# Three transformer blocks on one core: a cheaper root, an earlier start, an interleaved MLP start, and VectorE's later work queued behind each norm's root

## The chip, the cores and the metric

The kernel runs on one core of one Trainium2 chip (trn2). The metric is device time in microseconds (us); lower is better. TensorE (PE) does matmuls and transposes, VectorE (DVE) and ScalarE (ACT) do elementwise work, GpSimd (POOL) and SyncE (SP) here mostly issue transfers. Each engine has its own instruction queue and they meet through semaphores.

## The reference

One sequence of 512 tokens and 1024 features, in fp32, goes through three blocks: (1) latent attention with 8 heads and a gated short convolution side by side, then a gated MLP and a per-layer embedding gate; (2) retention with 4 heads and a squared-ReLU MLP; (3) banded attention with 16 heads and another squared-ReLU MLP. Ahead of, behind and inside these stand norms.

```
def _rmsnorm(x, g):
    y = x * lax.rsqrt(jnp.mean(x * x, axis=-1, keepdims=True) + EPS)
    return y * g
# block 1
z = rmsnorm(x, mix_pre_norm) @ w_in               # latents c_q, c_kv, rope keys, convolution inputs
q = rmsnorm(c_q, q_norm) @ w_uq;  kv = rmsnorm(c_kv, kv_norm) @ w_ukv
a = causal_attention(q, kv);  c = short_gated_conv(z)
m = concat(rmsnorm(a, attn_group_norm), rmsnorm(c, conv_group_norm))
x = x + rmsnorm(m @ w_out, mix_post_norm)
h = rmsnorm(x, ffn_pre_norm)
x = x + rmsnorm((silu(h @ w_gate) * (h @ w_up)) @ w_down, ffn_post_norm)
x = x + sigmoid(x @ w_ple_gate) * rmsnorm(p @ w_ple_proj, ple_norm)
# blocks 2 and 3, i = 0, 1
hn = rmsnorm(h, mix_norm_g[i])
h = h + (retention(hn) if i == 0 else chunk_attention(hn))   # retention norms each of its 4 heads
h = h + square(relu(rmsnorm(h, mlp_norm_g[i]) @ w1[i])) @ w2[i]
return rmsnorm(h, final_norm_g)
```

## The kernel before

**Layout.** Activations are kept transposed, features on partitions and the 512 tokens along the free axis. A product runs over eight 128-feature slices of its input. Every fp32 product is made of three matmuls of rounded parts (`mm3`, L147 to L150): L148 high x high, L149 low weight x high activation, L150 high weight x low activation. So a stream of matmuls at L148, L149, L150 is the body of the kernel; only L149 needs the low part `wl` of the weights.

**Weights.** A weight tile is 128 x 1024 fp32. SP loads it (`load_weights`, L134); ACT rounds it to `wh` (L111); DVE subtracts to get `wl` (L108, "the split"). Tiles `wr`, `wh` and `wl` are triple buffered. The two split instructions carry a priority 80 ahead (`HW = 80`).

**Order.** PE's order is written by hand: products are generators that yield after every `mm3` (a "unit" of three matmuls), and `pull(gen, n)` puts n units at that place in PE's queue. On the other engines a scheduler orders the instructions by priority when the program is built, and each queue then runs in that order.

**Norms.** `Norm` sums squares over the features (`square`: ACT squares, DVE adds). `column()` has PE transpose the sum in 128x128 pieces (L240), and `root()` (L245 to L260) makes the inverse root on DVE: one reduction (L247) and eleven small instructions, the last at L259. `spread()` has PE broadcast the result back over partitions (L265), and ACT copies it to `rb`. Between `column()` and `spread()` the code pulls a few units of the next product so that PE has work while DVE makes the root; new weight tiles that begin in this stretch are loaded, and split, by the instructions written there. A `SplitNorm` does the two 256-token halves one after the other.

**Places named below.** The first norm (start of the program), the two norms of the latents (their columns stand directly one after the other), the attention's norm, the two halves of the norm behind the output projection, the norm ahead of the gated MLP, the two halves of the norm behind it, the norm ahead of retention, retention's four head norms, the norms ahead of MLP 0, of the banded attention and of MLP 1, and the two halves of the last norm.

Of the kernel before, what the change touches and what calls it, by code (L numbers as in the profile page):

```python
# [14 lines left out]
P = 128  # L15
# [17 lines left out]
LAT = (6, 6, 12, 6, 5, 8, 2)  # L33
HID = (0, 9)
N_RET = (8, 5)
N_MLP = ((9, 8), (9, 5))
N_CH = (14, 12)
GG = (6, 7, 6)
FIN = (5, 8)
CO = (4, 11)  # L40
PER2 = (10,) * 8 + (13, 10, 9) + (10,) * 5 + (3,)

BIG = 1.0e30
# [17 lines left out]
def kernel(  # L61
# [29 lines left out]
    def small(n=NT, dt=F32, tag="sm"):  # L91
        return spool.tile([P, n], dt, tag=tag, name="small", bufs=12 if tag == "sm" else 4)
# [11 lines left out]
    def add(out, a, b):  # L104
        dve.tensor_tensor(out=out, in0=a, in1=b, op=ALU.add)  # L105
# [60 lines left out]
    def load4(src, n, acts=None, prepare=None, start=0, pool=None):  # L166
        out = []
        for kk in range(start, start + n):
            w = weight_tiles(pool)
            for k in range(2):  # L170
                load_weights(w, src[kk * P:(kk + 1) * P, :], slice(k * T, (k + 1) * T))
                if prepare is not None:
                    acts.append(prepare(2 * kk + k))
            out.append(w[1:])
        return out
# [41 lines left out]
    class Norm:  # L217


        def __init__(self, n, t0=0, nt=NT, acc=None):  # L220
            self.n, self.nt = n, nt
            self.tok = slice(t0 * P, (t0 + nt) * P)
            self.acc, self.r, self.col = acc, None, None
            self.waiting = []

        def square(self, src):
            w = self.nt * P
            if self.acc is None:
                self.acc = tmp()[:, :w]
                act.activation(self.acc, src, AF.Square)  # L230
            else:
                t = tmp()[:, :w]
                act.activation(t, src, AF.Square)  # L233
                add(self.acc, self.acc, t)

        def column(self):
            ps = bank()
# [5 lines left out]

        def root(self, ps):

            a, na, u, h, y, w = (small(dt=d, tag=g)[:, :self.nt] for d, g in ((F32, "sm"),) * 4 + ((I32, "smi"), (F32, "sm")))
            dve.tensor_reduce(out=a, in_=ps.rearrange("p (t f) -> p t f", f=P)[:, :self.nt, :], op=ALU.add, axis=AX.X)  # L247
            dve.tensor_scalar(a, a, 1.0 / self.n, EPS, ALU.mult, ALU.add)
            dve.tensor_scalar(y, a.bitcast(I32), -0.5, 1595932665.0, ALU.mult, ALU.add)
            dve.tensor_scalar(na, a, -0.703952253, None, ALU.mult)  # L250
            y = y.bitcast(F32)
            mul(u, y, y)
            mul(u, u, na)
            dve.scalar_tensor_tensor(out=y, in0=u, scalar=0.703952253 * 2.38924456, in1=y, op0=ALU.add, op1=ALU.mult)
            mul(u, y, y)
            mul(h, u, a)
            dve.tensor_scalar(w, y, 0.375, None, ALU.mult)
            dve.scalar_tensor_tensor(out=h, in0=h, scalar=-10.0 / 3.0, in1=h, op0=ALU.add, op1=ALU.mult)
            dve.scalar_tensor_tensor(out=w, in0=h, scalar=5.0, in1=w, op0=ALU.add, op1=ALU.mult)  # L259
            self.col = w  # L260

        def spread(self, sbuf=True):
            ps = bank()[:, :self.nt * P]
# [17 lines left out]
        def run(self, gen, a=10, b=8):  # L281
            pull(gen, a)
            self.column()
            pull(gen, b)
            self.spread()

    class SplitNorm:
# [128 lines left out]
    for kt in range(KT):  # L416
        t = const.tile([P, T], F32, name=f"x{kt}", tag=f"x{kt}")
        xs.append(t)

    warm = small(1)  # L420
    dve.memset(warm, 0.0)
    copy(warm, warm)
    ident = const.tile([P, P], F32, name="ident", tag="ident")


# [27 lines left out]
    with tc.tile_pool(name="m1", bufs=1) as m1, tc.tile_pool(name="pt1", bufs=1) as ptp:  # L453
# [3 lines left out]

        n_x = Norm(D)
        hn = []
        nc.gpsimd.dma_start(gn, gains)  # L460
        act.dma_start(xs[0], xT[:P, :])

        def first_in(kt):
            if kt > 0:
# [127 lines left out]
        pull(fill, LAT[2])  # L592
        n_lat[0].column()
        n_lat[1].column()
        pull(fill, LAT[3])
        for i in (1, 0):
            n_lat[i].spread()
            nm = ("q_norm", "kv_norm")[i]
# [12 lines left out]
        att = [m1.tile([P, T], F32, name=f"att{i}", tag=f"att{i}") for i in range(4)]  # L611
        wq = [None]
        qs = {}
        n_att = Norm(512)

        def project(h):
            if h == 2:
# [58 lines left out]
        def mla_head(h):  # L676
            def done(po):
                join(att[h // 2][64 * (h % 2):64 * (h % 2) + 64, :], po)
                if h % 2:
                    n_att.square(att[h // 2])  # L680
            return Head(qs.pop(h), keys[h // 2 % 2][h % 2], slice(0, P), causal, 96 ** -0.5, vps, h * P, done, True)

        first = project(0)
# [13 lines left out]
        attention(8, mla_head, mf, lambda h: per[h] if h < 6 else PER[h - 6], ptp, PER[2])  # L697
        pull(mf, OUT[0])
        n_att.column()
        drain(mf)  # L700


        heads = []
        for i in range(4):
            heads.append(split_gain(att[i], g_("attn_gn", i)))

        def out_unit(mt, ps, w, tok):
            yield from units(ps, w, K8[mt % 2 * 4:mt % 2 * 4 + 4], heads, tok=tok)
# [20 lines left out]
                    yield from out_unit(5 + k, ps3[k], ws[k], tok)  # L729

        out = att_out()
        pull(out, OUT[1])
        n_att.spread()
        pull(out, 32 + W_OUT[0] - OUT[1])
        n_post.halves[0].column()
        drain(out)

    ff = tc.tile_pool(name="ff", bufs=3, reuse_waits="tile")
    ffp = ff.__enter__()
# [10 lines left out]
    def boundary(norm, ys, gname, nxt, fill, counts, src, acts, loaded):  # L750

        a, b = norm.halves
        pull(fill, counts[1])
        a.spread(False)
        post_norm_add(a, ys, gname, nxt)
        pull(fill, counts[2])
        banks = [bank() for _ in range(4)]
        first = units4(banks, src, acts, loaded=loaded, tok=a.tok, pool=ffp)
        pull(first, counts[3])
        b.column()  # L760
        pull(first, counts[4])
        b.spread(False)
        post_norm_add(b, ys, gname, nxt)
        drain(first)
        drain(fill)
        return banks, units4(banks, src, acts, loaded=loaded, tok=b.tok)
# [41 lines left out]
    for nh in (8, 8, 6):  # L808
        hid = []
        if h0 == 0:  # L810
            for i in range(2):
                n_x.then(lambda i=i: hidden(hid, banks[i], banks[2 + i]))
            gen = hidden_group(hid, range(2, nh))
            n_x.run(gen, *HID)
            drain(gen)
        else:
            drain(hidden_group(hid, range(h0, h0 + nh)))
        last = h0 + nh == 22
        for mt in range(KT - 3 if last else KT):
            w = weights(rows(w_down, mt, h0, nh), nh * P)  # L820
            ps = bank()
            drain(units(ps, w, K8[:nh], hid))
            if h0 == 0:
                y = ffp.tile([P, T], F32, name=f"f{mt}", tag=f"f{mt}", bufs=1)
                copy(y, ps)
                accs.append(y)
            else:
                add(accs[mt], accs[mt], ps)
            if last:
                n_post.square(accs[mt])  # L830
        if last:
# [12 lines left out]

            drain(down_last(n_post.halves[0]))
            second = down_last(n_post.halves[1])
            pull(second, DOWN[0])
            n_post.halves[0].column()
            drain(second)
        h0 += nh  # L850

    es_t.append(pair())
# [42 lines left out]
    def mlp(i, now, nxt):  # L895
# [8 lines left out]
            hid.append(pr)  # L904

        def group(hid, grp):
            for j in range(8):
                w = weights(rows(m_w1, i * 32 + grp * 8 + j))
                ps = bank()
                yield from units(ps, w, K8, hn)  # L910
                norm.then(lambda ps=ps: square_relu(hid, ps))
                yield
# [22 lines left out]
    def finish(hid, ws):  # L935
# [33 lines left out]
        second = product(b)  # L969
        pull(second, FIN[0])  # L970
        a.column()
        pull(second, FIN[1])
        out = [f32(pair()) for _ in range(KT // 2)]
        output(a, out)
        drain(second)
# [6 lines left out]
    with tc.tile_pool(name="m2", bufs=1, reuse_waits="tile") as m2:  # L982
# [112 lines left out]
        for h in range(4):  # L1095
            if h % 2 == 0:
                ys = []
            vps = values(h)
            pts = retain(h)
            gnorm, os_ = Norm(T), []  # L1100
            gg = gates(h, gnorm, os_, ys)
            pull(gg, GG[0])
            os_ += outputs(vps, pts, gnorm)
            pull(gg, GG[1])
            gnorm.column()
            pull(gg, GG[2])
# [237 lines left out]
```

## Time and profile before

| | |
|---|---|
| three runs | 2006.85, 2009.34, 2009.49 us; median 2009.34 |
| profiled execution | 2007.66 us |
| its span, from first to last instruction | 2005.9 us |
| PE busy | 1967.7 us |
| DVE busy | 1193.7 us |
| ACT busy | 804.8 us |
| mean granted TensorE clock | 0.996 |

The profiled execution's own time is its span and what lies around it. Busy is the time in which an engine executed an instruction; PE's gaps are the difference to the span. The granted clock is 1 at TensorE's full rate (2.4 GHz) and 0.5 at half (1.2 GHz).

### The profile page before, as it was taken

The numbers are of one execution on the slowest core, as the hardware profiler recorded it, in microseconds if no ns is written. First come the engines' busy times: TensorE is split into PE (matmuls) and PEld (weight loads), VectorE is DVE, ScalarE is ACT, GpSimd is POOL, SyncE is SP. The second block draws the span as 40 slices with busy tenths as digits, with TensorE's granted clock in tenths as the row PEclk, the third lists the DMA queues.
The fourth block names the chain that finished last, engine by engine and source line by source line (L and its number), as shares of the span: only waits on it lengthen the run. The fifth ranks groups of instructions, "written<-read, shape, count | busy, mean of one in ns | idle before, by whom it ended". The sixth has DMA issues, their size and how long they took to land.

```text
span 2005.9 us, 23888 instructions
## 1 busy us (share of the span) xinstructions
PE 1967.7 (98%) x9340; PEld 1642.8 (82%) x9340; DVE 1193.7 (60%) x2167; ACT 804.8 (40%) x1298; POOL 10.3 (1%) x22
## 2 busy tenths in 40 slices
PE   8999899999999999999999999999999999999997
PEld 7787888888888788888888888888888878888887
DVE  7978963343469665635566354455598975444354
ACT  5776442332235344333443222223476753222232
POOL 1000000000000000000000000000000000000000
PEclk9999999999999999999999999999999999999999
DMA  5122223233241222222223233323222233233331
GB/s 181 60 65 85 85 86 104 95 95 95 95 129 65 100 75 79 99 99 74 79 95 95 94 95 97 103 95 95 100 85 80 67 107 95 95 95 96 103 95 64
DMA packets 58785, 185.31 MB, mean 92 GB/s; under 512 B 6784, under 2 KB 10000, under 8 KB 58672
## 3 DMA queue, kind: packets, MB, share of 16 engines
q1 hardware_dynamic: 53648, 175.76, 27.3%
q10 hardware_dynamic: 4688, 7.60, 1.3%
q8 instruction: 73, 1.20, 0.3%
q0 software_dynamic: 336, 0.42, 0.1%
q14 instruction: 40, 0.33, 0.1%
HBM read 181.56 MB, written 2.20 MB: 92 GB/s over the span
## 4 chain that ended last, share of the span: by engine, by line
PE 86%; DVE 9%; ACT 3%; issue 1%; DMA 0%; POOLq 0%; POOL 0%; ACTq 0%; DVEq 0%
PE bank L148 28%; PE bank L150 28%; PE bank L149 28%; DVE wl L108 2%; DVE tmp L105 1%; PE bank L360 1%; ACT tmp L328 1%; DVE pair L108 1%; ACT pair L111 1%; PE bank L341 1%; DVE tmp L326 1%; DVE pt L108 1%; ACT wh L111 1%; DVE x L105 0%; DVE pair L121 0%
## 5 line engine op out<-in xcount | busy, mean ns | idle before, releaser
L148 PE MATMUL bank<-pair,wh 128*128 128x512 f32 (+1 forms) x2550 | 979.9, 384 | 9.9 <-ACT pair L120 9.9
L150 PE MATMUL bank<-pair,wh 128*128 128x512 f32 (+1 forms) x2550 | 971.0, 381 | 1.8 <-DVE pair L121 1.5
L149 PE MATMUL bank<-pair,wl 128*128 128x512 f32 (+1 forms) x2550 | 969.5, 380 | 0.0
L111 ACT ACTIVATE wh<-wr 128x1024 fp32r<-128x1024 f32 (+4 forms) x354 | 353.1, 999 | 902.8 <-PE bank L150 654.6
L148 PEld LDWEIGHTS bank<-pair,wh 128*128 128x128 f32 x2550 | 480.9, 189 | 97.2 <-ACT pair L120 11.1
L150 PEld LDWEIGHTS bank<-pair,wh 128*128 128x128 f32 x2550 | 480.5, 188 | 97.0 <-DVE pair L121 3.8
L149 PEld LDWEIGHTS bank<-pair,wl 128*128 128x128 f32 x2550 | 481.0, 189 | 86.5
L108 DVE TENSOR_TENSOR wl<-wr,wh 128x1024 fp32r<-128x1024 f32 (+4 forms) x354 | 405.5, 1146 | 152.9 <-ACT wh L111 152.0
L102 DVE TENSOR_TENSOR tmp<-bank,rb 128x512 f32<-128x512 f32 (+1 forms) x140 | 94.4, 677 | 243.5 <-PE bank L150 238.8
L105 DVE TENSOR_TENSOR x<-x,bank 128x512 f32<-128x512 f32 (+1 forms) x99 | 66.2, 670 | 212.3 <-PE bank L150 212.2
L111 ACT ACTIVATE pair<-tmp 128x512 fp32r<-128x512 f32 (+1 forms) x188 | 118.5, 631 | 103.7 <-DVE tmp L1083 26.1
L108 DVE TENSOR_TENSOR pair<-tmp,pair 128x512 fp32r<-128x512 f32 (+1 forms) x156 | 106.7, 686 | 11.7 <-ACT pair L111 10.8
L105 DVE TENSOR_TENSOR tmp<-tmp 128x512 f32<-128x512 f32 (+1 forms) x107 | 68.2, 641 | 37.2 <-ACT tmp L233 36.7
L148 PE MATMUL bank<-wh,pair 128*128 128x512 f32 x200 | 79.2, 396 | 0.3 <-ACT tmp L111 0.3
L150 PE MATMUL bank<-wl,pair 128*128 128x512 f32 x200 | 78.0, 390 | 0.0
L149 PE MATMUL bank<-wh,pair 128*128 128x512 f32 x200 | 77.9, 389 | 0.0
L328 ACT ACTIVATE tmp<-tmp,small 128x512 f32<-128x512 f32 (+1 forms) x96 | 53.3, 556 | 28.8 <-DVE small L326 27.5
L108 DVE TENSOR_TENSOR pt<-bank,pt 128x512 fp32r<-128x512 f32 (+1 forms) x96 | 42.7, 484 | 10.0 <-ACT pt L111 9.8
L901 DVE SCALAR_TENSOR_TENSOR tmp<-tmp 128x512 f32<-128x512 f32 x64 | 44.2, 692 | 2.1
L120 ACT ACTIVATE pair<-x,gn 128x512 fp32r<-128x512 f32 (+1 forms) x56 | 36.2, 653 | 19.9 <-DVE x L105 18.9
L148 PEld LDWEIGHTS bank<-wh,pair 128*128 128x128 f32 x200 | 37.6, 188 | 7.9 <-ACT tmp L111 0.7
L150 PEld LDWEIGHTS bank<-wl,pair 128*128 128x128 f32 x200 | 37.5, 188 | 7.9
(151 smaller groups left out, 1221.5 us busy)
## 6 DMA issues: line engine op xcount, KB each, us to landing
wr<-in_m_w_dram SPq DMA_DIRECT2D x128, 512.0 KB, 3.7
wr<-in_r_qkg_dram SPq DMA_DIRECT2D x32, 512.0 KB, 3.5
wr<-in_w_gate_dram SPq DMA_DIRECT2D x20, 512.0 KB, 3.5
wr<-in_w_up_dram SPq DMA_DIRECT2D x20, 512.0 KB, 3.5
wr<-in_w_down_dram SPq DMA_DIRECT2D x16, 512.0 KB, 3.5
wr<-in_r_v_dram SPq DMA_DIRECT2D x16, 512.0 KB, 3.4
wr<-in_r_out_dram SPq DMA_DIRECT2D x16, 512.0 KB, 3.6
wr<-in_a_qk_dram SPq DMA_DIRECT2D x16, 512.0 KB, 3.5
```

The source lines that it names most:

```text
L102: dve.tensor_tensor(out=out, in0=a, in1=b, op=ALU.mult)
L105: dve.tensor_tensor(out=out, in0=a, in1=b, op=ALU.add)
L108: dve.tensor_tensor(out=out, in0=a, in1=b, op=ALU.subtract)
L111: act.activation(out, a, AF.Copy)
L120: act.activation(dst[:, 0, tok], src[:, tok], AF.Copy, scale=gain)
L148: pe.matmul(out, lhsT=ah, rhs=bh, start=start, stop=False)
L149: pe.matmul(out, lhsT=al, rhs=bh, start=False, stop=False)
L150: pe.matmul(out, lhsT=ah, rhs=bl, start=False, stop=stop)
L326: dve.tensor_tensor_reduce(out=s[:, :n], in0=ps[:, :n], in1=self.strip[:, T - n:T], scale=-self.scale, scalar=3.0e38, op0=ALU.add, op1=ALU ...
L328: act.activation(s[:, :n], s[:, :n], AF.Exp, bias=self.mx[:, col], scale=-1.0, accum_out=self.sm[:, col])
L341: pe.transpose(pt[:, j * P:(j + 1) * P], s[:, j * P:(j + 1) * P], ident)
L901: dve.scalar_tensor_tensor(out=t, in0=t, scalar=0.0, in1=t, op0=ALU.max, op1=ALU.mult)
```

## The change

1. **Start.** The gains `gn` and the first slice of x are now the first two transfers of ACT's queue (the gains were GpSimd's). The first weight piece is loaded and split as 128 + 384 columns with the first activation's preparation between. Eight matmuls of a zero tile (`IDLE = 8`) stand ahead of PE's first real one.
2. **Root.** `root()` has nine instructions instead of twelve; EPS goes into the sum of squares.
3. **MLP.** The first two tiles of each MLP's first group alternate unit by unit (14 units), and the second MLP's pulls are (14, 6) instead of (9, 5).
4. **Order.** `with norm.first():` is `tc.issue_after(root's last step)`: all that the block writes for DVE stands in DVE's queue behind the last instruction of that root. The blocks enclose the pull between `column()` and `spread()`.
5. **Heads.** The four products of the attention's output with its gain (`split_gain`, one ACT and one DVE instruction each) are made as each pair of heads ends, not together behind the fill.

```
-N_MLP = ((9, 8), (9, 5))
+N_MLP = ((9, 8), (14, 6))
+IDLE = 8
...
     def load4(src, n, acts=None, prepare=None, start=0, pool=None):
...
+                if prepare is not None and kk + k == 0:
+                    load_weights(w, src[:P, :], slice(0, P))
+                    acts.append(prepare(0))
+                    load_weights(w, src[:P, :], slice(P, T))
+                    continue
...
         def square(self, src):
...
-                add(self.acc, self.acc, t)
+                if self.eps:
+                    add(self.acc, self.acc, t)
+                else:
+                    dve.scalar_tensor_tensor(out=self.acc, in0=self.acc, scalar=self.n * EPS / P, in1=t,
+                                             op0=ALU.add, op1=ALU.add)
+                    self.eps = True
...
         def root(self, ps):
-            (12 instructions)
+            dve.tensor_reduce(out=s, in_=ps..., op=ALU.add, axis=AX.X)
+            dve.tensor_scalar(y, s.bitcast(I32), -0.5, 1595932665.0 + half, ALU.mult, ALU.add)
+            y = y.bitcast(F32)
+            stt(out=u, in0=y, scalar=-0.703952253 * 0.375 / n, in1=y, op0=ALU.mult, op1=ALU.mult)
+            mul(u, u, s)
+            stt(out=z, in0=u, scalar=0.375 * 0.703952253 * 2.38924456, in1=y, op0=ALU.add, op1=ALU.mult)
+            stt(out=u, in0=z, scalar=64.0 / (9.0 * n), in1=z, op0=ALU.mult, op1=ALU.mult)
+            mul(u, u, s)
+            stt(out=u, in0=u, scalar=-10.0 / 3.0, in1=u, op0=ALU.add, op1=ALU.mult)
+            self.last = stt(out=w, in0=u, scalar=5.0, in1=z, op0=ALU.add, op1=ALU.mult).ins
...
+        def first(self):
+            return tc.issue_after(self.last)
...
         def run(self, gen, a=10, b=8):
             pull(gen, a)
             self.column()
-            pull(gen, b)
+            with self.first():
+                pull(gen, b)
             self.spread()
...
+    act.dma_start(gn, gains)
+    act.dma_start(xs[0], xT[:P, :])
...
+    for _ in range(IDLE):
+        pe.matmul(zero, lhsT=idle[:, :P], rhs=idle[:, :T], start=True, stop=True)
...
         n_lat[0].column()
         n_lat[1].column()
-        pull(fill, LAT[3])
+        with n_lat[1].first():
+            pull(fill, LAT[3])
...
                 if h % 2:
                     n_att.square(att[h // 2])
+                    heads.append(split_gain(att[h // 2], g_("attn_gn", h // 2)))
...
         n_att.column()
-        drain(mf)
-        heads = []
-        for i in range(4):
-            heads.append(split_gain(att[i], g_("attn_gn", i)))
+        with n_att.first():
+            drain(mf)
```

The same `with` stands around the pull or drain behind `column()` in `out` (the attention's output), in `boundary` (both halves), in the last tiles of the gated MLP's down product, in retention's heads and at the last norm's first half. The norm ahead of MLP 1 and that ahead of MLP 0 go through `run`.

Two places of the order show it. First the first norm on DVE. `wl_418` before is the low part of the weight tile that PE reaches after seven matmuls of the fill behind this norm's column; after the change it is `wl_428`. Before, it stands 21 rows ahead of the root's reduction, between small instructions of the rope tables (`a2_298` to `a5_301`):

```order
L105 TENSOR_TENSOR a4_300<-a4_300,a3_299 128x64
L493 TENSOR_SCALAR a2_298<-a5_301 128x64
L108 TENSOR_TENSOR wl_418<-wr_416,wh_417 128x1024
L494 TENSOR_SCALAR a2_298<-a2_298 128x64
L496 SCALAR_TENSOR_TENSOR a3_299<-a5_301,a2_298 128x64
```

and the tile after it (`wl_474`, now `wl_484`) directly ahead of the reduction, so that no split waits for the root. After the change the nine instructions of the root come first, and the split behind them:

```order
L264 TENSOR_REDUCE small_406<-bank_401 128x4
L266 TENSOR_SCALAR small_408<-small_406 128x4
L268 SCALAR_TENSOR_TENSOR small_407<-small_408 128x4
L103 TENSOR_TENSOR small_407<-small_407,small_406 128x4
L270 SCALAR_TENSOR_TENSOR small_409<-small_407,small_408 128x4
L271 SCALAR_TENSOR_TENSOR small_407<-small_409 128x4
L103 TENSOR_TENSOR small_407<-small_407,small_406 128x4
L273 SCALAR_TENSOR_TENSOR small_407<-small_407 128x4
L274 SCALAR_TENSOR_TENSOR small_410<-small_407,small_409 128x4
L109 TENSOR_TENSOR wl_428<-wr_426,wh_427 128x1024
L109 TENSOR_TENSOR wl_484<-wr_482,wh_483 128x1024
```

Both splits moved from ahead of the reduction to behind the root's last step (L274). PE's queue at the same place, after the change (its order there is that of before): the column's four transposes, seven matmuls, and then the first that reads `wl_428`:

```order
L254 MATMUL bank_401<-ident_102,tmp_286 128x128 x4
L149 MATMUL bank_382<-pair_251,wh_377 128x512
L150 MATMUL bank_382<-pair_251,wl_378 128x512
L151 MATMUL bank_382<-pair_251,wh_377 128x512
L149 MATMUL bank_382<-pair_259,wh_377 128x512
L150 MATMUL bank_382<-pair_259,wl_378 128x512
L151 MATMUL bank_382<-pair_259,wh_377 128x512
L149 MATMUL bank_432<-pair_122,wh_427 128x512
L150 MATMUL bank_432<-pair_122,wl_428 128x512
```

Nothing moved in these PE rows; what moved is when `wl_428` can be ready. The second place is the latents' two norms on DVE, after the change. The second root (the first one's nine rows stand directly ahead of these) stands ahead of three splits, the first of which (`wl_553`) PE reads after one matmul:

```order
L264 TENSOR_REDUCE small_537<-bank_532 128x4
L266 TENSOR_SCALAR small_539<-small_537 128x4
L268 SCALAR_TENSOR_TENSOR small_538<-small_539 128x4
L103 TENSOR_TENSOR small_538<-small_538,small_537 128x4
L270 SCALAR_TENSOR_TENSOR small_540<-small_538,small_539 128x4
L271 SCALAR_TENSOR_TENSOR small_538<-small_540 128x4
L103 TENSOR_TENSOR small_538<-small_538,small_537 128x4
L273 SCALAR_TENSOR_TENSOR small_538<-small_538 128x4
L274 SCALAR_TENSOR_TENSOR small_541<-small_538,small_540 128x4
L109 TENSOR_TENSOR wl_553<-wr_551,wh_552 128x1024
L109 TENSOR_TENSOR wl_634<-wr_632,wh_633 128x1024
L109 TENSOR_TENSOR wl_654<-wr_652,wh_653 128x768
```

Before, `wl_551` (now `wl_553`) stood directly behind the first norm's root, a norm earlier. The number of matmuls between the column's transposes and the first one that reads a split moved behind the root, counted in PE's order in the same way: first norm 7; latents 1; attention's norm 7; norm behind the output projection 13 and 10 (of 256 tokens); ahead of the gated MLP 1; behind it 19 and 19 (of 256 tokens); ahead of retention 1; each retention head 10; ahead of MLP 0 22; ahead of the banded attention 8; ahead of MLP 1 7.

## Rows read from the trace of the kernel before

**Rows 1.** The page's busy times: time, share of the span, instructions.
```profile
PE 1967.7 (98%) x9340; PEld 1642.8 (82%) x9340; DVE 1193.7 (60%) x2167; ACT 804.8 (40%) x1298; POOL 10.3 (1%) x22
```

**Rows 2.** PE's waits: line, releaser: us in total, times, longest.
```profile
PE bank L265 <- DVE small L259: 8.1, 7, 2.3
...
PE bank L240 <- DVE tmp L105: 4.0, 3, 2.3
...
PE bank L150 <- DVE pair L121: 1.5, 3, 0.9
```

**Rows 3.** Stretches: length, busy of each engine, granted clock, DMA share, GB/s.
```profile
6.46:11.60 5.14, 5.14 (x12) 3.98 (x13) 4.74 (x8) 5.04 (x10) 0.00 (x0) 1.00 0.95 309
81.90:86.90 5.00, 3.01 (x18) 2.08 (x17) 4.00 (x11) 4.97 (x15) 0.00 (x0) 1.00 0.02 5
170.90:178.10 7.20, 4.41 (x24) 3.74 (x25) 5.62 (x25) 5.20 (x14) 0.00 (x0) 1.00 0.44 146
219.90:226.70 6.80, 4.55 (x20) 3.81 (x20) 6.23 (x24) 2.13 (x6) 0.00 (x0) 0.75 0.24 77
...
597.50:604.30 6.80, 4.43 (x27) 3.82 (x28) 6.18 (x20) 2.87 (x6) 0.00 (x0) 1.00 0.48 155
1645.00:1650.00 5.00, 3.54 (x12) 2.64 (x12) 2.79 (x5) 2.30 (x3) 0.00 (x0) 0.66 0.26 100
1646.60:1650.00 3.40, 3.40 (x11) 2.51 (x12) 1.98 (x3) 1.40 (x2) 0.00 (x0) 0.50 0.01 5
```

**Rows 4.** Timeline of the start: start, duration, engine, line, what, idle before.
```profile
1.28 0.74 POOL L460 DMA_DIRECT2D gn<-in_gains_dram  x1 [0.82 <-POOLq L1332]
...
4.37 0.63 ACT L111 ACTIVATE wh<-wr 128x512 fp32r<-128x512 f32 x1 [1.68 <-DMA wr<-in_w_lat_dram]
...
5.68 0.72 ACT L120 ACTIVATE pair<-x,gn 128x512 fp32r<-128x512 f32 x1 [0.69 <-DMA gn<-in_gains_dram]
...
6.46 0.80 PE L148 MATMUL bank<-pair,wh 128*128 128x512 f32 x1 [6.46 <-ACT pair L120]
```

**Rows 5.** Timeline of DVE and PE around the first norm's root.
```profile
26.70 1.22 DVE L108 TENSOR_TENSOR wl<-wr,wh 128x1024 fp32r<-128x1024 f32 x1
...
35.48 0.69 DVE L247 TENSOR_REDUCE small<-bank 128x4 f32<-128x512 f32 x1 [2.11 <-PE bank L240]
...
36.90 0.39 PE L149 MATMUL bank<-pair,wl 128*128 128x512 f32 x1
...
37.60 0.16 DVE L258 SCALAR_TENSOR_TENSOR small<-small 128x4 f32<-128x4 f32 x1
...
37.80 0.16 DVE L259 SCALAR_TENSOR_TENSOR small<-small 128x4 f32<-128x4 f32 x1
...
38.01 1.23 DVE L108 TENSOR_TENSOR wl<-wr,wh 128x1024 fp32r<-128x1024 f32 x1
```

**Rows 6.** Timeline of DVE and PE at the latents' two norms.
```profile
48.66 0.69 DVE L247 TENSOR_REDUCE small<-bank 128x4 f32<-128x512 f32 x1 [2.38 <-PE bank L240]
...
49.13 0.39 PE L149 MATMUL bank<-pair,wl 128*128 128x512 f32 x1
...
53.99 1.09 PE L265 MATMUL bank<-ident,small 128*128 128x128 f32 x8 [0.82 <-DVE small L259]
```

**Rows 7.** Timeline of DVE and PE ahead of retention.
```profile
658.87 0.69 DVE L247 TENSOR_REDUCE small<-bank 128x4 f32<-128x512 f32 x1 [0.75 <-PE bank L240]
...
658.90 0.39 PE L149 MATMUL bank<-pair,wl 128*128 128x512 f32 x1
```

**Rows 8.** Timeline of DVE and PE at retention's first head norm.
```profile
718.68 0.69 DVE L247 TENSOR_REDUCE small<-bank 128x4 f32<-128x512 f32 x1 [1.52 <-PE bank L240]
...
720.80 0.39 PE L149 MATMUL bank<-pair,wl 128*128 128x512 f32 x1
```

**Rows 9.** Timeline of DVE and PE ahead of MLP 0.
```profile
1060.45 0.68 DVE L247 TENSOR_REDUCE small<-bank 128x4 f32<-128x512 f32 x1
...
1064.13 0.39 PE L149 MATMUL bank<-pair,wl 128*128 128x512 f32 x1
```

More of the change, by code (lines that the diff above doesn't have):

```diff
@@ L223, in __init__ @@
             self.acc, self.r, self.col = acc, None, None
+            self.eps = acc is not None
             self.waiting = []
@@ L244, in root @@
         def root(self, ps):
[L246 to L250, printed above, removed]
-            y = y.bitcast(F32)
[L252 to L259, printed above, removed]
+            s, u, y, z, w = (small(dt=d, tag=g)[:, :self.nt] for d, g in
+                             ((F32, "sm"), (F32, "sm"), (I32, "smi"), (F32, "sm"), (F32, "sm")))
+            stt, n = dve.scalar_tensor_tensor, self.n
+            dve.tensor_reduce(out=s, in_=ps.rearrange("p (t f) -> p t f", f=P)[:, :self.nt, :], op=ALU.add, axis=AX.X)
+            half = (n.bit_length() - 1) * 2.0 ** 22
+            dve.tensor_scalar(y, s.bitcast(I32), -0.5, 1595932665.0 + half, ALU.mult, ALU.add)
+            y = y.bitcast(F32)
+            stt(out=u, in0=y, scalar=-0.703952253 * 0.375 / n, in1=y, op0=ALU.mult, op1=ALU.mult)
[5 more added lines that the diff above has]
+            self.last = stt(out=w, in0=u, scalar=5.0, in1=z, op0=ALU.add, op1=ALU.mult).ins
             self.col = w
+        def first(self):
+            return tc.issue_after(self.last)
         def spread(self, sbuf=True):
@@ L422 @@
     copy(warm, warm)
+    idle = wpool.tile([P, 8 * P], F32R, tag="wl", name="idle")
+    dve.memset(f32(idle[:, :T]), 0.0)
+    zero = bank()
+    for _ in range(IDLE):
+        pe.matmul(zero, lhsT=idle[:, :P], rhs=idle[:, :T], start=True, stop=True)
     ident = const.tile([P, P], F32, name="ident", tag="ident")
@@ L459 @@
         hn = []
-        nc.gpsimd.dma_start(gn, gains)
-        act.dma_start(xs[0], xT[:P, :])
         def first_in(kt):
@@ L613 @@
         qs = {}
-        n_att = Norm(512)
+        n_att, heads = Norm(512), []
         def project(h):
@@ L731 @@
         out = att_out()
-        pull(out, OUT[1])
+        with n_att.first():
+            pull(out, OUT[1])
         n_att.spread()
@@ L735 @@
         n_post.halves[0].column()
-        drain(out)
+        with n_post.halves[0].first():
+            drain(out)
     ff = tc.tile_pool(name="ff", bufs=3, reuse_waits="tile")
@@ L752, in boundary @@
         a, b = norm.halves
-        pull(fill, counts[1])
+        with a.first():
+            pull(fill, counts[1])
         a.spread(False)
@@ L760, in boundary @@
         b.column()
-        pull(first, counts[4])
+        with b.first():
+            pull(first, counts[4])
         b.spread(False)
@@ L848 @@
             n_post.halves[0].column()
-            drain(second)
+            with n_post.halves[0].first():
+                drain(second)
         h0 += nh
@@ L906, in group @@
         def group(hid, grp):
-            for j in range(8):
+            if grp == 0:
+                two = [(bank(), weights(rows(m_w1, i * 32 + j))) for j in range(2)]
+                parts = [units(ps, w, K8, hn) for ps, w in two]
+                for _ in range(2 * KT - 2):
+                    next(parts[_ % 2])
+                    yield
+                for (ps, _), part in zip(two, parts):
+                    drain(part)
+                    norm.then(lambda ps=ps: square_relu(hid, ps))
+                    yield
+            for j in range(2 if grp == 0 else 0, 8):
                 w = weights(rows(m_w1, i * 32 + grp * 8 + j))
@@ L971, in finish @@
         a.column()
-        pull(second, FIN[1])
+        with a.first():
+            pull(second, FIN[1])
         out = [f32(pair()) for _ in range(KT // 2)]
@@ L1105 @@
             gnorm.column()
-            pull(gg, GG[2])
+            with gnorm.first():
+                pull(gg, GG[2])
             gnorm.spread()
```

## The prediction

> **What bounds the kernel now.** I read the page's busy times first. PE is busy 98% of the span [rows 1]; the rest is 38 us (2005.9 − 1967.7). So what the change takes from DVE's work is worth nothing by itself: it counts only where PE waits. PE's waits come next. Those that the change could shorten are few: the broadcast waits for the root's last step for 8.1 us in seven places, the column waits for the sum of squares for 4.0 us, and L150 waits 1.5 us for activations [rows 2]. Third, the stretches around the longest gaps, for TensorE's clock. Of the five longest gaps within the program (length less PE's busy time: 1.99, in several pieces; 2.79; 2.25; 2.37; 1.46), two were followed by a stretch at half clock (1.2 GHz): the mean of 0.75 over 6.8 us and 0.66 over 5 us are both half clock for 3.4 us [rows 3]. In such a stretch half of the 3.4 us is lost: 1.7 us. The start is slow too: 12 matmuls in 5.14 us, 0.43 us each, although the clock column reads 1.00 there [rows 3]; in the 0.50 stretch they stand as far apart, elsewhere 0.23 us (below). I read it as half clock from the first matmul on, after an idle engine.
>
> **The change part by part.**
>
> *Start.* The first matmul stands at 6.46, behind the first activation's high part (5.68 + 0.72), which waited 0.69 us for the gains; those are issued by GpSimd at 1.28 [rows 4]. First in ACT's queue they come earlier, and the high part can follow the first weight piece's rounding (4.37 + 0.63, for a quarter of the columns less): about 0.5 us earlier (0 to 0.7). The zero matmuls put work on PE in the idle time before. No row shows such matmuls; if they count, the 12 slow ones lose up to 12 × 0.2 = 2.5 us of delay, if not, nothing. I take 1.7 us, one slow stretch as priced above. Start: −2.2 (−3.2 to 0). By the Trainium skill (TensorE: Matmul & The Clock Gate, What's actually happening) the default state is throttled and activity releases it; by that rule the whole 2.5 us would go and the sum below would be 0.8 us less. The half-clock matmuls at the start agree with its first half, and no row here bears on whether zeros count.
>
> *Root.* In the first norm it takes from 35.48 to 37.96, and its dependent small steps are 0.20 us apart (37.60, 37.80) [rows 5]. The chain is one step shorter: 2.29 us instead of 2.48. The other two removed instructions had filled gaps. Alone it is worth 0.2 us wherever PE waits for the root.
>
> *The order.* This decides. Before, the first norm's next weight tile was split at 26.70, 9 us ahead of the root, and PE used it at 36.90 [rows 5]. After, the split stands behind the root's last step. The root can't start before PE has made the column, and that stands in PE's order where it stood. So the low part is ready at the reduction's start + 2.29 (root) + 1.2 (split, 1.22 or 1.23 [rows 5]) = 3.5 us later. PE reaches L149 of that tile at a time the code fixes. With one matmul in hand this is 0.03 us behind the reduction's start [rows 7], with ten 2.12 us [rows 8]: 0.232 us for each. PE can't pass the waiting matmul, so the stall is 3.5 − 0.03 − 0.232 (n − 1), with n from the order shown ahead:
>
> - first norm, n = 7: 35.48 + 3.5 − 36.90 = 2.1 [rows 5].
> - latents: two roots in a row from 48.66, then the split: 48.66 + 2 × 2.29 + 1.2 − 49.13 = 5.3; the 0.82 wait of the broadcast goes [rows 6].
> - attention's norm, n = 7: 2.1. Its reduction should come 0.4 us earlier without the head products ahead of it; I leave that out here.
> - norm behind the output projection. Half-width matmuls count half (0.116) and the split needed first is of 512 columns (0.6 less): with 13 and 10 in hand 1.5 and 1.9; three and four other instructions of DVE stand within the roots, for which I add 0.4 and 0.8: 1.9 and 2.7.
> - ahead of the gated MLP, n = 1: 3.5, and 0.1 for an addition within: 3.6.
> - behind it, 19 and 19 of half width: 0.8 each; within the second root stand nine other instructions, one a split: +1.8. Together 0.8 + 2.6.
> - ahead of retention, n = 1: 3.5 [rows 7].
> - retention's four head norms, n = 10: 718.68 + 3.5 − 720.80 = 1.4 each, 5.6 [rows 8].
> - ahead of MLP 0, n = 22: 1060.45 + 3.5 is before 1064.13: none [rows 9].
> - ahead of the banded attention, n = 8: 1.9; ahead of MLP 1, n = 7: 2.1.
>
> Sum of stalls: 2.1 + 5.3 + 2.1 + 1.9 + 2.7 + 3.6 + 0.8 + 2.6 + 3.5 + 5.6 + 1.9 + 2.1 = 34.2 us. Against it stand the waits that go. While PE stalls, the root ends, so of the 8.1 us of the broadcast's waits only the last norm's 2.3 stays, less 0.2 [rows 2]: −6.0. The free root lets the sum of squares behind the output projection come earlier: its column's wait of about 2.3 [rows 2, 3], and the slow stretch behind it, 1.7 [rows 3], go: −4.0. Splits that move out of the chain of x ahead of retention shrink L150's 1.5 us and its neighbours: −1.6 [rows 2].
>
> *MLP.* Alternating two tiles gives the first activation's successors twice the time; the 1.46 us gap ahead of MLP 1 and the slow stretch behind it [rows 3] go: −3.2. If only the first tile's second activation is covered, −1.5.
>
> *Heads.* Four pairs of about 0.7 us on ACT (as the first activation's high part, 0.72 [rows 4]) and as much on DVE move into the attention, which PE already waits on there (the gaps at 81.90 and 170.90 [rows 3]). I take 0; it could cost up to 1.5 or gain as much.
>
> Without the clock: 34.2 − 2.2 − 6.0 − 4.0 − 1.6 − 3.2 = +17.2.
>
> *The clock.* Ten of the new stalls last 1.9 us or more (all but the 0.8 and the retention heads). Three, of 3.5 to 5.3, are longer than any gap within the program before, and I give each a half-clock stretch of 1.7 us. The other seven lie in the span 1.46 to 2.79 in which two gaps of five had one [rows 3]; I take about half, 3.5. Together 6.5 × 1.7 = 11 (0 to 17; the longest stall could have two).
>
> Sum: 2007.66 + 17.2 + 11 = 2036. That profiled execution is 1.7 us below the median of its runs, 2009.34; the sum stays with its own time.
>
> The rule that bears on the order: the Trainium skill (PSUM — Partial Sum Buffer, Engine vs sequencer instructions) says that the queues of ScalarE, VectorE and GpSimdE are strict FIFO. If a ready split could pass the waiting root, the time would be the 1991 of the third rival; the reduction rows, with only instructions that the order puts ahead of them before, agree with the rule.
>
> **The rivals.**
>
> 1. *The clock holds.* Most stalls are near 2 us, and gaps of 2.37 and 2.79 us were followed by full clock [rows 3]; against it stands that 1.46 sufficed once. Then 2007.66 + 17.2 = 2025.
> 2. *All go cold, and the queue behind.* Every long stall costs 1.7, the longest twice: +18.7 instead of 11. Behind each root stand three or four splits, 3.7 to 4.9 us of DVE at 1.22 each; the instructions that free banks for PE wait behind them, at some norms for about 0.5 us more. Together 2007.66 + 17.2 + 18.7 + 2 = 2045.
> 3. *Faster.* The deferred splits are not needed early. That is how it is at MLP 0, where 22 matmuls, 3.7 us, lie between [rows 9]. It decides from n = 1 + 3.47 / 0.232 = 16 on. If PE had such cover everywhere, stalls and clock would fall away: 2007.66 − 17.0 = 1991. Against it are the rows at n = 1, 7 and 10 [rows 5 to 8]: the order leaves no such cover.
> 4. *The gains are larger or the stalls smaller by half.* If the scheduler's earlier chains shift the roots ahead by 1.5 us at each of twelve norms, 17 us would go: 2019 with the clock's share, 2008 without, which is no change. The column stands in PE's own order, so little can shift.
>
> **How the numbers follow.** The forecast has 0.68, rival 1 0.13, rival 2 0.12, rival 3 0.04, rival 4 0.03 (the no-change end). The time is that of the forecast, 2036. Low: no clock falls, the start at its best (−1.0) and stalls 15% smaller (−5): 2019. High: rival 2 with 2 us for the heads and rounding: 2047. The range leaves out rivals 3 and 4 and the tails, below 2 in 10. A measurement of this kernel can tell about 0.2%, 4 us, from no change: faster 0.04, same 0.03, slower 0.93.
>
> **What would show it.** In the changed kernel's waits of PE a new row stands at the top: L150 (the low-part product, L149 before) waiting for DVE's split (L109), about 34 us in some fifteen places, the longest about 5.3 at the latents. The waits of the broadcast shrink to the last norm's 2.1. Half-clock stretches follow at least the three longest stalls. The head norms of retention show 1.4 us each, and MLP 0 none. PE's first real matmul stands near 5.9, and its first twelve start 0.23 apart if zeros count. The prediction is wrong if that row is short or missing, or if roots take much less than 2.29 us.

## The result and the profile after

The changed kernel takes 2037.5 us (median; 2035.55 to 2038.79) against 2008.84 (2006.85 to 2009.49): ratio 1.0142, interval 1.0128 to 1.0156, so 1.4% slower. Its profiled execution has a span of 2033.7 us, 27.8 more than before, at a mean granted clock of 0.991.

PE's waits in the changed kernel (line, releaser: us in total, times, longest) answer to [rows 2]:

```profile
PE bank L150 <- DVE wl L109: 30.5, 14, 5.0
...
PE bank L149 <- ACT pair L121: 3.0, 3, 1.4
PE bank L254 <- DVE tmp L106: 2.1, 2, 1.5
PE bank L284 <- DVE small L274: 2.1, 1, 2.1
...
PE bank L151 <- DVE wl L109: 1.7, 1, 1.7
```

The first and last rows are new: PE waits 32.2 us in 15 places for the split of a weight tile. The broadcast's wait for the root (now L284 and L274) has shrunk from 8.1 us to the last norm's 2.1, the column's (L254) from 4.0 to 2.1, and the wait for the activations' low part is gone. The first norm on the timeline, DVE and then PE, answers to [rows 5]:

```profile
33.22 0.69 DVE L264 TENSOR_REDUCE small<-bank 128x4 f32<-128x512 f32 x1 [2.50 <-PE bank L254]
33.94 0.17 DVE L266 TENSOR_SCALAR small<-small 128x4 int32<-128x4 int32 x1
...
35.33 0.16 DVE L274 SCALAR_TENSOR_TENSOR small<-small 128x4 f32<-128x4 f32 x1
35.41 1.23 DVE L109 TENSOR_TENSOR wl<-wr,wh 128x1024 fp32r<-128x1024 f32 x1
```

```profile
34.41 0.40 PE L149 MATMUL bank<-pair,wh 128*128 128x512 f32 x1
36.69 0.50 PE L150 MATMUL bank<-pair,wl 128*128 128x512 f32 x1 [1.89 <-DVE wl L109]
```

The root takes 33.22 to 35.49, 2.27 us; the split starts at 35.41, 0.08 before the last step's end, and PE goes on 0.05 us behind the split's end. The reader should see one more thing here: the view counts 1.89 us as idle, from the end of the matmul before (34.41 + 0.40), but an undelayed matmul would have started 0.23 us after it. The delay is 36.69 − 34.41 − 0.23 = 2.05 us. Each wait in this view is about 0.16 us short of what it costs: 32.2 + 15 x 0.16 = 34.6 us.

The latents, with two roots in a row:

```profile
48.59 0.69 DVE L264 TENSOR_REDUCE small<-bank 128x4 f32<-128x512 f32 x1 [2.73 <-PE bank L254]
...
50.79 0.68 DVE L264 TENSOR_REDUCE small<-bank 128x4 f32<-128x512 f32 x1
...
52.97 3.22 DVE L109 TENSOR_TENSOR wl<-wr,wh 128x1024 fp32r<-128x1024 f32 x3
54.24 0.79 PE L150 MATMUL bank<-pair,wl 128*128 128x512 f32 x1 [5.01 <-DVE wl L109]
...
54.83 0.63 PE L151 MATMUL bank<-pair,wh 128*128 128x512 f32 x1
55.26 0.63 PE L149 MATMUL bank<-pair,wh 128*128 128x512 f32 x1
```

Three splits stand in one block behind the second root, and PE needs only the first. Behind the stall the matmuls start 0.43 us apart: half clock. The stretches with the longer stalls (length, busy of PE, PEld, DVE, ACT, POOL, granted clock, DMA share, GB/s) answer to [rows 3]:

```profile
34.00:44.00 10.00, 8.11 (x38) 6.39 (x37) 6.84 (x16) 3.78 (x5) 4.22 (x8) 1.00 0.38 118
48.00:60.00 12.00, 6.99 (x26) 5.49 (x25) 7.04 (x21) 0.84 (x1) 0.00 (x0) 0.72 0.34 117
203.00:210.00 7.00, 5.12 (x16) 3.74 (x15) 4.99 (x10) 1.06 (x1) 0.00 (x0) 0.76 0.39 135
231.00:238.00 7.00, 4.15 (x21) 3.06 (x21) 6.20 (x20) 3.26 (x8) 0.00 (x0) 1.00 0.11 37
243.00:251.00 8.00, 5.48 (x33) 5.27 (x33) 5.19 (x17) 1.37 (x2) 0.00 (x0) 0.79 0.37 125
268.00:278.00 10.00, 5.71 (x17) 4.29 (x16) 6.66 (x15) 0.92 (x1) 0.00 (x0) 0.66 0.36 122
624.00:631.00 7.00, 4.47 (x38) 4.26 (x37) 7.00 (x19) 3.78 (x8) 0.00 (x0) 1.00 0.51 161
674.00:684.00 10.00, 6.73 (x21) 5.12 (x19) 5.40 (x12) 0.56 (x1) 0.00 (x0) 0.66 0.46 154
...
1440.00:1447.00 7.00, 5.33 (x24) 4.10 (x23) 4.47 (x10) 1.06 (x1) 0.00 (x0) 1.00 0.46 156
1680.00:1688.00 8.00, 6.12 (x23) 4.62 (x22) 4.52 (x10) 2.26 (x3) 0.00 (x0) 0.79 0.50 170
```

What is missing to full clock in a row (12 us x 0.28, 7 x 0.24, and so on) comes to 3.4 + 1.7 + 1.7 + 3.4 + 3.4 + 1.7 = 15.3 us, nine pieces of 1.7. Not all of this is lost, because at the three longest stalls (5.0, 4.3, 3.3 us) the clock falls while PE still waits. The same columns, for the end of the first of these stalls and for the half-clock work behind all three:

```profile
52.11:54.23 2.12, 0.00 (x0) 0.00 (x0) 1.98 (x7) 0.00 (x0) 0.00 (x0) 0.50 0.00 0
54.24:58.94 4.70, 4.70 (x11) 3.73 (x12) 1.95 (x2) 0.00 (x0) 0.00 (x0) 0.50 0.67 221
...
272.79:277.38 4.59, 4.59 (x11) 3.62 (x12) 2.21 (x2) 0.00 (x0) 0.00 (x0) 0.50 0.67 227
...
677.73:683.57 5.84, 5.84 (x14) 4.64 (x15) 2.21 (x2) 0.00 (x0) 0.00 (x0) 0.50 0.74 246
```

Half of the time in which PE works at half clock is lost: (4.70 + 4.59 + 5.84) / 2 = 7.6 us. Of the seven stalls of 1.7 to 2.5 us three were followed by 3.4 us at half clock, 1.7 us lost each. Together the clock costs 12.7 us. The four stalls of 1.2 us and the one of 0.8 have none behind them.

### The profile page after: what moved, and what is told of

The parts are those of the page before. It is cut to its first block, busy times and chain, and to the rows that moved or that the text cites. A ratio compares the mean times of both kernels' runs of the same rounds, so it can differ in the third digit from the quotient of the medians.

```text
span 2033.7 us, 23831 instructions
## 1 busy us (share of the span) xinstructions
PE 1979.5 (97%) x9348; PEld 1650.2 (81%) x9348; DVE 1192.9 (59%) x2106; ACT 804.7 (40%) x1299; POOL 9.7 (0%) x21
## 4 chain that ended last, share of the span: by engine, by line
PE 88%; DVE 8%; ACT 3%; issue 1%; DMA 0%; POOL 0%; POOLq 0%; DVEq 0%; SPq 0%; ACTq 0%
PE bank L150 28%; PE bank L151 28%; PE bank L149 28%; DVE wl L109 1%; PE bank L380 1%; PE bank L361 1%; DVE tmp L106 1%; DVE pair L109 1%; ACT tmp L348 1%; ACT pair L112 0%; DVE small L264 0%; ACT wh L112 0%; DVE x L106 0%; DVE tmp L346 0%; PE bank L284 0%
## 5 line engine op out<-in xcount | busy, mean ns | idle before, releaser
L150 PE MATMUL bank<-pair,wl 128*128 128x512 f32 (+1 forms) x2550 | 973.9, 382 | 30.5 <-DVE wl L109 30.5
L112 ACT ACTIVATE wh<-wr 128x1024 fp32r<-128x1024 f32 (+5 forms) x355 | 353.4, 997 | 921.6 <-PE bank L151 647.5
L150 PEld LDWEIGHTS bank<-pair,wl 128*128 128x128 f32 x2550 | 483.1, 189 | 122.4 <-DVE wl L109 35.5
L109 DVE TENSOR_TENSOR wl<-wr,wh 128x1024 fp32r<-128x1024 f32 (+5 forms) x355 | 403.6, 1144 | 142.6 <-ACT wh L112 142.3
L109 DVE TENSOR_TENSOR pair<-tmp,pair 128x512 fp32r<-128x512 f32 (+1 forms) x156 | 106.8, 686 | 12.7 <-ACT pair L112 11.8
L150 PE MATMUL bank<-wh,pair 128*128 128x512 f32 x200 | 77.9, 390 | 0.0
L106 DVE TENSOR_TENSOR tmp<-tmp 128x512 f32<-128x512 f32 (+1 forms) x89 | 56.4, 634 | 17.0 <-ACT tmp L241 16.1
L361 PEld LDWEIGHTS bank<-ident,tmp 128*128 128x128 f32 x240 | 30.5, 140 | 16.5 <-ACT tmp L352 6.4
```

The source lines that it names most:

```text
L109: dve.tensor_tensor(out=out, in0=a, in1=b, op=ALU.subtract)
L112: act.activation(out, a, AF.Copy)
L150: pe.matmul(out, lhsT=al, rhs=bh, start=False, stop=False)
L361: pe.transpose(pt[:, j * P:(j + 1) * P], s[:, j * P:(j + 1) * P], ident)
```

## The experiments

**Nothing held.** Only `first()` is undone.

```
         def first(self):
-            return tc.issue_after(self.last)
+            return nullcontext()
```

> The changed kernel with the order part alone undone: nothing is held behind a root, the other parts stay. Theory (the held splits make PE wait, and the waits let the clock fall): all 14 waits of the low-part product on a split go, 32 us, with nine half-clock stretches, about 15 us less the two that the kernel before had. Some waits of the broadcast come back, about 6 us. About 2002 us, between 1997 and 2007: faster than before, by the start (2.7), the interleaved MLP (about 3) and the shorter root (about 1). Rival (the other parts cost something too, or the stalls are only moved): above 2009.

2000.82 us (1999.12 to 2002.22), ratio to the kernel before 0.9965 (0.9952 to 0.9978). PE's waits:

```profile
PE bank L284 <- DVE small L274: 7.0, 6, 2.1
PE bank L361 <- ACT tmp L352: 4.8, 4, 2.8
PE bank L254 <- DVE tmp L106: 3.4, 3, 1.7
PE bank L149 <- ACT pair L121: 2.1, 3, 0.9
```

No wait on a split is left, and the broadcast's waits are back. The order alone makes 2037.5 − 2000.8 = 36.7 us; all else in the change gains 7.

**The order alone**, added to the kernel before, behind its twelve-step root (`with ....first():` at the same places).

> The kernel before with the order part alone added: the same blocks are held behind the old twelve-step root. Theory: the same stalls as in the changed kernel, each about 0.2 us longer, and the half-clock stretches behind them; 2009 + 36 = 2045 us, between 2040 and 2050. Rival (the order costs only together with the earlier head products or the zero matmuls): below 2030.

2049.32 us (2048.92 to 2049.74), ratio 1.0209 (1.0194 to 1.0224): 41.5 us, inside the theory's range, near its upper end. The waits on the split are 33.6 us in 13 places and 1.9 in one, the clock 0.988:

```profile
PE bank L149 <- DVE wl L108: 33.6, 13, 5.1
...
PE bank L150 <- DVE wl L108: 1.9, 1, 1.9
```

So the cost needs neither the moved heads nor the zero matmuls.

**The first two splits free.** In each held block the first two loads are traced outside the hold.

```
+        held = hold[0]
+        free = held is not None and held.loads < 2
...
+        if free:
+            held.off()          # leaves tc.issue_after for this load
         sp.dma_start(raw[:, c], src[:, c])
         with tc.high_priority(offset=HW):
             copy(hi[:, c], raw[:, c])
             sub(lo[:, c], raw[:, c], f32(hi[:, c]))
+        if free:
+            held.on()
```

> The changed kernel, but in each held block the splits of the first two loads are traced outside the hold; the later splits and all other work stay behind the root. Theory: PE needs only the first split of a block within 16 matmuls, the next ones 25 or more matmuls later, so the stalls go as if nothing were held: within 4 us of the kernel with nothing held, and the roots run undisturbed, so perhaps 1 to 3 us below it. Rival (the other held work, sums, products with the inverse root, bank evacuations, costs as well): 5 us or more above the kernel with nothing held.

2003.22 us (2000.27 to 2005.86), ratio 0.9978 (0.9968 to 0.9987). The theory held in that nearly all of the 36.7 us goes; the further gain did not come. The broadcast's waits do shrink (7.0 to 4.4 us), but the column now waits 5.3 us for sums of squares, and PE 1.5 us for an activation's high part. Holding the rest gains nothing over holding nothing.

**Matmuls in hand.** In the changed kernel the column of retention's head norm h stands h units earlier, the broadcast where it was.

```
-            pull(gg, GG[1])
+            pull(gg, GG[1] - h)
             gnorm.column()
             with gnorm.first():
-                pull(gg, GG[2])
+                pull(gg, GG[2] + h)
```

> The changed kernel with the column of retention's four head norms put 0, 1, 2 and 3 units (0, 3, 6, 9 matmuls) earlier in PE's order, the broadcast staying where it is, so that 10, 13, 16 and 19 matmuls stand between the column and the first use of the held split. Theory: the stall falls by 0.232 us for each matmul in hand, from 1.2 us: 1.2, 0.5, 0 and 0; 3.1 us less than the changed kernel, about 2034. Rival (the wait is on something else than the root's distance, for example the transfer or the other splits): four stalls of 1.2 us as before, 2037.

2033.95 us (2032.58 to 2035.39), 3.5 less than the changed kernel. The first two heads in PE's timeline:

```profile
745.61 0.49 PE L150 MATMUL bank<-pair,wl 128*128 128x512 f32 x1 [1.18 <-DVE wl L109]
```

```profile
824.18 0.50 PE L150 MATMUL bank<-pair,wl 128*128 128x512 f32 x1 [0.53 <-DVE wl L109]
```

At the third (16 in hand) PE runs on as the split ends, and at the fourth there is no wait either; the waits on the split fell from 15 places to 13. One matmul in hand is worth 0.22 us ((1.18 − 0.53) / 3), and the cover ends at 16, as the third rival's price said.

**The hold at the head norms alone**, in the kernel with nothing held.

> The kernel with nothing held, with the hold put back at retention's four head norms alone. Theory: four stalls of 1.2 us and no half-clock stretch behind them: 2000.8 + 4.8 = 2005.6 us, 2004 to 2007.5. Rival (each stall costs its clock too, 1.7 us more): 2012.

2006.13 us (2004.67 to 2008.85): + 5.3. Four waits of 4.8 us together, and no half-clock stretch behind any of the four. Stalls of 1.2 us cost themselves alone.

**The hold at the latents alone**, likewise.

> The kernel with nothing held, with the hold put back at the latents' two norms alone. Theory: one stall of 5.0 us, the broadcast's wait of 0.8 gone, and one or two half-clock stretches of 1.7 us behind it: 2000.8 + 5.9 to 7.6, so 2006.7 to 2008.4. Rival (the clock is no part of it): 2005.

2006.67 us (2004.75 to 2010.18): + 5.9, at the lower edge of the theory's range and too near the rival's 2005 to decide by time. The trace decides: when the stall of 5.0 us ends, PE works at half clock for 4.50 us and loses half of them, 2.3 us.

```profile
53.95:58.45 4.50, 4.50 (x11) 3.53 (x12) 1.95 (x2) 0.00 (x0) 0.00 (x0) 0.50 0.77 221
```

**Work in the stalls.** The changed kernel with zero matmuls ahead of the waiting product at eleven places. They add zero to the bank.

```
+    def zeros(out, w):
+        n = pad.pop(id(w[1]), (0, None))[0]
+        for _ in range(4 * n):      # 2 * n in the second run
+            pe.matmul(out[:, :P], lhsT=nil, rhs=nil, start=False, stop=False)
...
         pe.matmul(out, lhsT=ah, rhs=bh, start=start, stop=False)
+        if w is not None and not tok:
+            zeros(out, w)           # n is 1 to 20, at the held tile's first use alone
         pe.matmul(out, lhsT=al, rhs=bh, start=False, stop=False)
+        if tok:                     # where the weights' low part is read by the third matmul
+            zeros(out, w)
```

> The changed kernel with zero matmuls put into PE's queue directly ahead of the waiting low-part product at eleven places (4 to 80 of 128 columns, together about 22 us of PE, each less than the stall it stands in); they add zero to the bank. Theory (half-clock stretches come from the stalls): the nine stretches of 3.4 us go, 15 us, while the stalls keep their ends; about 2023 us, 2019 to 2028, mean clock near that of the kernel before. Rival (the clock falls for another reason, or the zero matmuls delay PE): 2035 or more.

2044.46 us (2043.86 to 2044.89): a miss. The clock came back to 0.998, but a zero matmul of 128 columns took 0.115 us (43.6 / 380), twice what I had taken, and the 380 of them outlasted the stalls:

```profile
L143 PE MATMUL bank<-nil 128*128 128x128 f32 x380 | 43.6, 273 | 0.0
```

> The changed kernel with half as many zero matmuls in the stalls as the first try, 2 to 40 of 128 columns; there one took 0.115 us, so together they now take 22 us and fit into the stalls that they stand in. Theory: the stalls keep their ends, the half-clock stretches go: 2037.5 - 15 = 2023 us, 2019 to 2028, with the waits on the split shortened by what the zeros fill. Rival (the clock has nothing to do with these stalls): 2035 or more.

2028.2 us (2025.4 to 2029.92), 9.3 less than the changed kernel, 0.2 above the range. The same stretches as above now run at full clock:

```profile
48.00:60.00 12.00, 11.41 (x77) 10.14 (x76) 7.04 (x21) 0.84 (x1) 0.00 (x0) 1.00 0.25 81
203.00:210.00 7.00, 6.42 (x37) 5.42 (x36) 6.08 (x14) 1.06 (x1) 0.00 (x0) 1.00 0.17 51
...
268.00:279.00 11.00, 10.24 (x64) 8.99 (x63) 6.37 (x15) 1.57 (x3) 0.00 (x0) 1.00 0.44 143
674.00:684.00 10.00, 9.36 (x49) 7.85 (x49) 7.44 (x12) 1.66 (x2) 0.00 (x0) 1.00 0.45 157
```

The stalls' ends have not moved (zeros of 22.4 us and remaining waits of 11.8 fill them), so the 9 us are the clock's. That is less than 12.7; the zeros and what is left of the waits come to 34.2 us where the waits alone were 32.2, which explains 2 us, and 9.3 + 2 is 11.3. This profiled execution itself gained less, 5.6 us (2033.7 − 2028.1), and its rows say why. It has half clock at a place without a held split, behind a wait of 2.8 us in the attention that the changed kernel has too, with full clock behind it there; PE works in 5.9 us of that half clock and loses 2.9:

```profile
170.00:190.00 20.00, 17.18 (x77) 13.75 (x76) 13.37 (x42) 14.11 (x33) 0.00 (x0) 0.83 0.24 79
```

And its start ran at half clock where the changed kernel's did not (last section), so that the first norm's reduction starts at 34.78 instead of 33.22, 1.6 us later. 12.7 − 2 − 2.9 − 1.6 = 6.2, against 5.6.

**The other parts**, each taken out of the kernel with nothing held: the zero matmuls at the start (`IDLE`, tile and loop left out), the moved head products (back behind the fill), the alternating tiles of the MLPs (with the old pulls), the nine-step root (the old one in its place).

> The kernel with nothing held, without the eight zero matmuls at the start. Theory (they raise the clock ahead of the real work): the first twelve real matmuls stand 0.43 us apart again instead of 0.23 and the time rises by 2 to 2.5 us, to about 2003. Rival (the start waits for transfers and activations, and the faster matmuls only wait more): within 1 us of 2000.8.

2001.47 us (2000.01 to 2004.71): + 0.7, not to be told from nothing.

> The kernel with nothing held, with the four head products of the attention back in one place behind the fill. Theory: they are worth about 0 on the path in the attention, and 0.4 to 1 us at the attention's norm, whose root they stand in the way of: 2001 to 2002. Rival (split pair by pair they lengthen the attention's gaps): 1999 to 2000.

2002.8 us (2001.01 to 2003.92): + 2.0, more than the theory gave. The broadcast's waits rise from 7.0 to 8.1 us and the column's from 3.4 to 3.8.

> The kernel with nothing held, without the two alternating tiles at the start of each MLP and with the old pulls. Theory: the 1.46 us wait ahead of MLP 1 comes back, and with it a half-clock stretch of 1.7: about 2004. Rival (the wait was covered by something else in the change, or only its 1.5 us counts because the clock holds): 2001 to 2002.3.

2003.57 us (2001.99 to 2007.61): + 2.8, as the theory said. The wait for activations rises from 2.1 to 3.7 us: the 1.46 us ahead of MLP 1 are back, and so is the half clock behind them.

```profile
1643.60:1647.00 3.40, 3.40 (x11) 2.62 (x11) 1.91 (x3) 1.49 (x2) 0.00 (x0) 0.50 0.03 11
```

> The kernel with nothing held, with the old twelve-step root. Theory: six waits of the broadcast, each 0.2 us longer, about 1.2 us: 2002. Rival (the three instructions fewer also free VectorE for what PE waits for): 2003.5 or more; or none of it is on the path: 2001.

2003.63 us (2002.12 to 2004.73): + 2.8, where 1.2 was expected, so the rival's case. The broadcast's waits are 8.5 us (7.0 with the new root); the rest of it is not located.

The intervals of these four are about 0.1% wide to either side and overlap, so the single figures carry 2 us of doubt. Their sum, 8.3, stands beside the 7.0 that all gain together.

## Why the prediction was right

The forecast was 2036 us, and 2037.5 came.

*The order decides.* Shown: undone, 36.7 us go; added alone, 41.5 come. The waiting instruction is the one that was named, in 15 places, the longest 5.0 us (5.3 forecast). That the queue held back work that was ready can be read at the first norm. ACT had finished the tile's high part at 29.76 (28.70 + 1.06), and DVE then stood idle for 2.50 us ahead of the reduction at 33.22, with the split behind it in its queue:

```profile
28.70 1.06 ACT L112 ACTIVATE wh<-wr 128x1024 fp32r<-128x1024 f32 x1 [4.38 <-PE bank L151]
```

*The formula of the stalls.* It gave 34.2 us; the views show 32.2 of waiting, 34.6 of delay with the 0.16 us that each row leaves out. By place, as waits: first norm 1.89 (2.1), latents 5.01 (5.3), attention's norm 1.88 (2.1), output projection 1.70 and 2.52 (1.9, 2.7), gated MLP 4.29 (3.6), behind it 0.78 and 2.53 (0.8, 2.6), retention 3.27 (3.5), its heads 1.2 each (1.4), banded attention 1.67 (1.9), MLP 1 1.88 (2.1), MLP 0 none (none). With 0.16 us added, all but one lie within 0.15 us of the forecast. Only the norm ahead of the gated MLP was off, by 0.85 us (4.29 + 0.16 against 3.6, of which 0.1 was for an addition): there VectorE was still busy with additions when the column was ready, so the reduction itself came later, and one whole addition stands behind it:

```profile
266.65 2.29 DVE L106 TENSOR_TENSOR tmp<-tmp 128x512 f32<-128x512 f32 x3
268.86 0.68 DVE L264 TENSOR_REDUCE small<-bank 128x4 f32<-128x512 f32 x1
269.46 0.68 DVE L106 TENSOR_TENSOR tmp<-tmp 128x512 f32<-128x512 f32 x1
```

The slope was forecast as 0.232 us for a matmul in hand and measured as 0.22, with the end of the cover at 16.

*The clock.* Right in kind: with work in the stalls the stretches run at full clock. It was a little under-sized: 12.7 us in the profiled execution instead of 11. Two errors nearly cancel in it. The half-clock time at each of the three longest stalls was two stretches, not one; for the seven others half was right (three). But the forecast lets PE work through every stretch, and at the three longest stalls it stood idle for a part of it. The median gives 9.3 to 11.3 by the zeros. Half clock is not the order's alone: the kernel with nothing held has it too in its profiled execution, for 6.8 us ahead of retention (a mean of 0.62 from 651 to 660). That place and the attention have it in some profiled executions and not in others.

*The waits that go.* They were a little under-sized too. 34.6 + 12.7 is 47.3, and the span grew by 27.8, so 19.5 went, where 17.0 was forecast. The rows show: broadcast 6.0, column 1.9, L150's activations 1.5, the two slow stretches of before 3.4, the start 2.3 (the first norm's reduction at 33.22 instead of 35.48). Apart from the start, the waits for the activations' high part fell from 3.4 us to 1.6, the 1.46 ahead of MLP 1 among them; of before:

```profile
PE bank L148 <- ACT pair L120: 9.9, 4, 6.5
```

Together 16.9, and with 0.16 for each of the eleven waits that vanished 18.7; the last 0.8 us have no single row. The forecast of 2036 is this close because the clock's 1.7 us too few and these 2.5 us too few nearly cancel.

*The start.* The first real matmul came at 6.27, not near 5.9: it still waits for the first activation's high part (5.52 + 0.71), which now stands behind the second weight piece's rounding on ACT (5.09). In this execution the real matmuls started 0.23 us apart from the fourth on, and so the start gained 2.3 us, where 2.2 was forecast. That agreement is luck: the earlier matmul gave 0.2 instead of 0.5, and the clock stays a matter of chance (last section).

The faster rival fell by its own test: where 16 matmuls of full width are in hand the order costs nothing, and only MLP 0 has that many. The first rival, a clock that holds, fell by the 12.7 us. Against the second, only three of the seven shorter stalls went cold, and no row of PE's waits stands on an instruction that frees a bank behind the splits. The fourth needed gains of 34 us or stalls of half the size.

## What to carry to other kernels

Before holding an engine's work behind a dependent chain, count what the fastest engine has in hand at that place: here the chain and one split take 3.5 us and each matmul covers 0.23, so a held split needs 16 matmuls, and most places had 1 to 10. Moving a slow chain's interrupters out of its way gains the chain's own waits (here 6 us), but the interrupters may be what the critical engine needs next (here 35 us of stalls). Price a stall of the matmul engine with what its clock does afterwards: here stalls of 1.2 us cost themselves alone, and each of the twelve of 3.3 us and more, in four profiled executions, cost another 1.5 to 3.0 us.

## What the runs showed of the hardware

The eight zero matmuls at the start raise the clock in some executions and not in others. In the profiled executions of the eleven kernels that have them, the first real matmuls stood 0.23 us apart (from the fourth on) in five and 0.43 in six; in the three without, 0.43 each time. Two of the eleven, the kernel with nothing held and the one with the hold at the head norms alone, differ only at retention's head norms, 700 us later, and yet came out differently, so I put it down to chance. The first norm's reduction started at 32.98 to 33.44 in the five and from 34.65 on in the six: the difference is worth about 1.5 us. Here are the changed kernel, where they did,

```profile
1.50 3.40 PE L450 MATMUL bank<-idle 128*128 128x512 f32 x8 [1.50 <-DVE idle L447]
6.27 0.50 PE L149 MATMUL bank<-pair,wh 128*128 128x512 f32 x1 [1.37 <-ACT pair L121]
```

the kernel with the hold at the head norms alone, where they did as well,

```profile
1.50 3.78 PE L450 MATMUL bank<-idle 128*128 128x512 f32 x8 [1.50 <-DVE idle L447]
6.49 0.50 PE L149 MATMUL bank<-pair,wh 128*128 128x512 f32 x1 [1.21 <-ACT pair L121]
```

and the kernel with nothing held, where they didn't:

```profile
1.50 3.78 PE L450 MATMUL bank<-idle 128*128 128x512 f32 x8 [1.50 <-DVE idle L447]
6.11 0.80 PE L149 MATMUL bank<-pair,wh 128*128 128x512 f32 x1 [0.82 <-ACT pair L121]
```

The zeros end at 4.90, 5.28 and 5.28, and PE is idle until 6.27, 6.49 and 6.11. In the changed kernel 3.40 us means that some of the zeros ran at full clock already; but the duration does not tell the cases apart, since with 3.78 us the real matmuls stood 0.23 us apart in one kernel and 0.43 in the other. The first real matmul itself does: it lasted 0.50 us in the first two and 0.80 in the third. The Trainium skill (TensorE: Matmul & The Clock Gate, What's actually happening) says that activity releases the throttle; the five executions agree, and in the six the same activity just ahead did not.

A matmul of 128 columns with its own weight load took 0.115 us where one of 512 took 0.23: a quarter of the columns for half of the time.
